# Projections of the three-branch attention units issued as one line of quarters at equal distances, tied to the attention's products on both sides

## Chip, cores and metric

The kernel runs on one core of a Trainium2 chip. The metric is the device time of one execution in microseconds (us): 919.52 us, the median of three runs (917.04 to 920.32).

## What is computed

One decoder layer over 1,024 tokens of width 1,024, in fp32. Cut to what matters:

```python
h = rms_norm(x, g_pre) * (1 + scale) + shift
proj = h @ w_in                 # split into q_a, three k/v pairs, gates, z_a, q_b, kv_b, z_b, merge
o_cmp, p_cmp = compressed_attention(qa, kc, vc)
o_slc = selected_attention(qa, ks_, vs_, select_blocks(p_cmp))
o_win = banded_attention(qa, kw_, vw_, window=512)
o_a = g0 * o_cmp + g1 * o_slc + g2 * o_win          # mixer A: 8 heads, three branches
y_a = (merge_heads(o_a) * silu(z_a)) @ w_o_nsa
o_b = banded_attention(qb, kb_, vb_, window=128, sinks)   # mixer B: 8 heads, one branch
y_b = (merge_heads(o_b) * silu(z_b)) @ w_o_swa
y = (sigmoid(m_a) * y_a + sigmoid(m_b) * y_b) @ w_out     # m_a, m_b: the merge gates
x = x + gate * rms_norm(y, g_post)
```

With 16 blocks of 64 keys and 16 selected, the selected branch (`slc`) is full causal attention.

## The kernel before

**Products.** An fp32 product is made of three fp32r products: each operand is split into a high and a low part (`hh`, `hl` for the normed input, `wh`, `wl` for weights, `ph`, `pl` for probabilities), and high times high, low times high and high times low are added in PSUM. The input's parts stay in SBUF for the whole kernel, as 8 pieces of 128 channels by two halves of 512 tokens.

**Projections.** One projection half (`proj_half`, lines 172 to 190) makes 128 output channels for 512 tokens: 8 pieces times 3 matmuls of 512 columns (lines 181, 188, 189) into one PSUM bank with the tag `pj` (two banks). Its weights come as a block in two halves: SyncE loads 256 KB (`wraw`, three buffers), ScalarE casts the high part (L155), GpSimd subtracts the low part (L158); `wh` and `wl` have six buffers, three blocks. What comes out is Q (scaled, split, L479), K (L494), Z (the SiLU gate, through a tanh, L522, to DRAM) or a merge gate (a copy by ScalarE, L859, to DRAM: "spilled").

**Attention.** It runs in four units: mixer B, groups 0 and 1 (one branch), then mixer A, groups 0 and 1 (three branches: `slc`, `win`, `cmp`). A unit goes through 8 blocks of 128 queries, branch by branch. `scores` makes, for each of 4 heads, products of Q and K (lines 752, 755) in one of three `s` banks, from which VectorE adds distances and takes minima (L762, L768); ScalarE then takes the exponential (L774), and GpSimd scales the rows (L786). One task later, `weigh` turns each 128 by 128 piece of the rows of 4 heads with four PE transposes into a `pt` bank (L821; two banks); ScalarE casts the high part `ph` (L827), VectorE subtracts the low part `pl` (L828), and PE multiplies the values with `ph` (L829) and with `pl` (L832) into the single `pv` bank. For the compressed branch that is L794, L800, L801 and L805. `finish` takes the block's output from the bank (L841, L842), multiplies it by Z and stores it.

**The order.** A scheduler that estimates times sets each engine's order when the program is built; the code steers it with priorities and with order-only dependencies (`after`, `chain`) that cost no semaphore. Attention is recorded at high priority. `mark` notes, at each attention product, how many columns of attention have been recorded so far (`done`, in microseconds at 2,400 columns each). Projections are recorded between tasks: Q, K and Z at steps that `spread` gives out, and the 28 merge halves by the shares in `LATE`, the fractions of them that each unit takes. A projection half is bound on one side: its first matmul must stand behind the attention product that was marked 3 us (`AHEAD`) before its place. Nothing says where it must be done; its 24 matmuls stand where the scheduler finds them best.

After the attention come two merge blocks that were kept back, the two output projections with their gates, and the last product.

Of the kernel before, what the change touches and what calls it, by code (L numbers as in the profile page):

```python
# [7 lines left out]
F32 = mybir.dt.float32  # L8
# [6 lines left out]
P = 128  # L15
D = 1024
S = 1024
HS = 512
KC = D // P
NT = S // P  # L20
EPS = 1e-6
LATE = (0.1, 0.1, 0.2, 0.6)
WARM = (7, 14, 8, 4)
KEEP = 2
WBUFS = 6
AHEAD = 3
PRIO = 1500
# [40 lines left out]
def hybrid_kernel(tc, io, out):  # L68
# [10 lines left out]
    def bank(tag):  # L79
        return ps.tile([P, 512], F32, tag=tag, name=f"b_{tag}", bufs=BANKS[tag])  # L80
# [15 lines left out]
    done = [0.0]  # L96

    def mark(ins, columns):

        marks.append((done[0], ins))  # L100
        done[0] += columns / 2400
# [365 lines left out]
    Q = {}  # L467
# [48 lines left out]
    def z_block(name, half, w):  # L516

        t = proj_half(w, half, lambda: bank("pj"))
        if half == 0:
            spilled[name] = dram.tile([P, S], F32, name=f"sp_{name}", tag=f"sp_{name}")  # L520
        sp = kq.tile([P, HS], F32, name="sp", tag="sp", bufs=1)
        nc.scalar.activation(sp, t, AF.Tanh, scale=0.5)  # L522
        nc.vector.scalar_tensor_tensor(sp, sp, 1.0, t, ALU.add, ALU.mult)
        nc.sync.dma_start(spilled[name][:, half * HS : half * HS + HS], sp)
# [148 lines left out]
    def chunks(lo, hi):  # L673
# [6 lines left out]
        return res  # L680

    cmp_scores = {}

# [10 lines left out]
    def scores(mixer, g, i, br):  # L694
# [33 lines left out]
        for r in range(4):  # L728
            h = 4 * g + r
            if len(rows) < 4:  # L730
                q = Q[(mixer, h, half)][:, qo : qo + P]
# [58 lines left out]
    def weigh_pairs(g, pairs, pv):  # L790

        t = bank("pt")
        for p in range(2):
# [15 lines left out]
    def weigh(mixer, g, i, br, tiles, pv, first, last):  # L809
# [6 lines left out]
        todo = [((b - b0) * P, V[b][:, vi]) for b in range(b0, i + 1)]  # L816
        for n, (off, v) in enumerate(todo):
            v = v.rearrange("p a d -> p (a d)")
            t = bank("pt")
# [29 lines left out]

    late = []  # L850

    def add_spill(name):
        def block(half, w):
            if half == 0:
                w.extend(load_block(name))
                spilled[name] = dram.tile([P, S], F32, name=f"sp_{name}", tag=f"sp_{name}")
            t = proj_half(w, half, lambda: bank("pj"))
            sp = kq.tile([P, HS], F32, name="sp", tag="sp", bufs=1)
            nc.scalar.copy(sp, t)  # L859
            nc.sync.dma_start(spilled[name][:, half * HS : half * HS + HS], sp)  # L860

        w = []
        for half in range(2):
            late.append(lambda half=half: block(half, w))

    for n in SPILL:
        add_spill(n)
    late_done = [0]
    n_late = len(late)

# [10 lines left out]
    for u, (mixer, g) in enumerate(units):  # L881
# [11 lines left out]

        own = [] if u == 1 else k_fills(mixer, g, 1)
        spread(own + q_fills(mixer, g, 1), 0, 3 * nt // 8)
        if u + 1 < len(units):
            m2, g2 = units[u + 1]
            if u == 2:
                spread(z_fills(m2, g2), 3 * nt // 8, nt)
            nk = k_fills(m2, g2, 0) if m2 == "A" else []  # L900
            spread(nk + q_fills(m2, g2, 0), nt // 2, nt)
        prev = None
        pvs = {}
# [9 lines left out]
        for n, (i, br) in enumerate(tasks):  # L913
# [13 lines left out]
            now = done[0] - begun  # L927
            while late_done[0] < n_late:

                part = ((late_done[0] + 0.5) / n_late - sum(LATE[:u])) / LATE[u]  # L930
                if part > 1 or part * whole[u] > now:
                    break
                hold[0] = held(begun + part * whole[u] - AHEAD)
                late.pop(0)()
                late_done[0] += 1
        with tc.high_priority(offset=PRIO):
            second(prev)
    for f in late:
        f()
    hold[0] = None  # L940
# [243 lines left out]
```

## Time and profile before

| | |
|---|---|
| median of three runs | 919.52 us (917.04 to 920.32) |
| the profiled execution's own time | 919.45 us |
| its span, first to last instruction | 917.6 us |
| TensorE (PE) busy | 902.7 us, 98% |
| weight loads (PEld) busy | 755.5 us, 82% |
| VectorE / ScalarE / GpSimd busy | 553.5 / 504.0 / 355.0 us |

PE's matmuls overlap in the records (a matmul of 512 columns is listed with some 390 ns while the next starts 0.23 us after it), so PE's busy share hides short stops; the starts of consecutive rows and the waits of the weight loads show them. Mixer B's units lie between about 165 and 316 us, mixer A's between 316 and 714 us: group 0 until about 495, group 1 from there.

### The profile page before, as it was taken

What the parts mean: (1) busy time and instruction counts of PE and PEld (TensorE: products, weight loads), DVE (VectorE), ACT (ScalarE), POOL (GpSimd) and SP (SyncE); (2) the same over time, 40 slices, a digit from 0 to 9 for tenths busy, and PEclk for the clock granted to TensorE, in tenths of its full rate; (3) what the DMA queues carried; (4) which work ended last, traced back from release to release, by engine and by line L of the source; (5) the groups of instructions that cost most, each with busy time, mean ns of one, the idle gap of its engine ahead of it and who ended that gap; (6) DMA issues with size and microseconds to landing.
All of it is one profiled execution on the core that took longest, in us unless ns stands there. A gap on an engine that the chain in (4) does not pass through costs nothing.

```text
span 917.6 us, 14306 instructions
## 1 busy us (share of the span) xinstructions
PE 902.7 (98%) x4568; PEld 755.5 (82%) x4568; DVE 553.5 (60%) x1546; ACT 504.0 (55%) x1151; POOL 355.0 (39%) x422
## 2 busy tenths in 40 slices
PE   9999999999999999999999999999999999999997
PEld 7888888888888878878887888887887888887885
DVE  5866863475677866785575865565555372676322
ACT  5476722466776675675565765665645465441111
POOL 0000421465675865553443764534433276200000
PEclk9999999999999999999999999999999999999999
DMA  8962442332242311202101221121211587334432
GB/s 320 304 242 75 139 161 72 127 96 95 79 118 90 112 62 44 83 26 70 64 30 35 81 86 61 37 72 39 77 47 49 185 260 240 109 110 178 138 98 85
DMA packets 63868, 100.82 MB, mean 110 GB/s; under 512 B 7473, under 2 KB 24241, under 8 KB 63794
## 3 DMA queue, kind: packets, MB, share of 16 engines
q1 hardware_dynamic: 62640, 98.69, 32.8%
q10 hardware_dynamic: 1154, 1.23, 0.4%
q8 instruction: 36, 0.59, 0.3%
q14 instruction: 38, 0.31, 0.1%
HBM read 79.97 MB, written 19.92 MB: 109 GB/s over the span
## 4 chain that ended last, share of the span: by engine, by line
PE 91%; DVE 3%; ACT 2%; issue 1%; DMA 1%; POOL 1%; DVEq 0%; ACTq 0%; POOLq 0%
PE b_pj L188 12%; PE b_pj L189 12%; PE b_pj L181 12%; PE b_pt L821 7%; PE b_s L752 4%; PE b_s L755 4%; PE b_pv L832 4%; PE b_pv L829 3%; PE b_s L1069 1%; PE b_s L1067 1%; PE b_s L1068 1%; PE b_pt L288 1%; DVE pl L828 1%; PE b_s L204 1%; PE b_s L990 1%
## 5 line engine op out<-in xcount | busy, mean ns | idle before, releaser
L181 PE MATMUL b_pj<-hh,wh 128*128 128x512 f32 x528 | 209.1, 396 | 0.0
L189 PE MATMUL b_pj<-hh,wl 128*128 128x512 f32 x528 | 208.5, 395 | 0.0
L188 PE MATMUL b_pj<-hl,wh 128*128 128x512 f32 x528 | 207.6, 393 | 0.0
L158 POOL TENSOR_TENSOR wl<-wraw,wh 128x512 fp32r<-128x512 f32 x102 | 133.9, 1316 | 138.6 <-ACT wh L155 92.6
L828 DVE TENSOR_TENSOR pl<-b_pt,ph 128x512 fp32r<-128x512 f32 x162 | 110.0, 685 | 46.3 <-ACT ph L827 45.4
L827 ACT CAST ph<-b_pt 128x512 fp32r<-128x512 f32 x162 | 92.8, 584 | 64.8 <-PE b_pt L821 51.2
L189 PEld LDWEIGHTS b_pj<-hh,wl 128*128 128x128 f32 x528 | 99.3, 188 | 18.5
L188 PEld LDWEIGHTS b_pj<-hl,wh 128*128 128x128 f32 x528 | 99.3, 188 | 17.8
L181 PEld LDWEIGHTS b_pj<-hh,wh 128*128 128x128 f32 x528 | 99.3, 188 | 17.6
L786 POOL TENSOR_SCALAR ps<-ps,rr,gates 128x128 f32<-128x128 f32 (+7 forms) x64 | 53.2, 836 | 98.9 <-DVE rr L778 92.3
L752 PE MATMUL b_s<-kh,q 128*128 128x256 f32 (+6 forms) x272 | 88.4, 332 | 1.5 <-DVE minc L768 0.9
L774 ACT ACTIVATE ps<-ps,mins 128x256 f32<-128x256 f32 (+7 forms) x96 | 65.1, 679 | 36.9 <-DVE mins L762 35.9
L755 PE MATMUL b_s<-kl,q 128*128 128x256 f32 (+6 forms) x272 | 84.2, 316 | 0.0
L155 ACT CAST wh<-wraw 128x512 fp32r<-128x512 f32 x94 | 58.0, 619 | 40.8 <-PE b_pj L188 32.9
L774 ACT ACTIVATE pw<-pw,mins 128x256 f32<-128x256 f32 (+4 forms) x96 | 60.5, 632 | 30.9 <-DVE mins L762 28.2
L832 PE MATMUL b_pv<-pl,V 128*128 128x512 f32 x162 | 69.6, 430 | 2.5 <-DVE pl L828 2.0
L829 PE MATMUL b_pv<-ph,V 128*128 128x512 f32 x162 | 67.2, 415 | 0.9 <-ACT ph L827 0.7
L786 POOL TENSOR_SCALAR pw<-pw,rr,gates 128x640 f32<-128x640 f32 (+4 forms) x64 | 47.6, 746 | 40.9 <-DVE rr L778 36.9
L843 POOL TENSOR_TENSOR ot<-ot,zt 64x512 f32<-64x512 f32 x32 | 41.3, 1290 | 49.3 <-DVE ot L842 40.0
L752 PEld LDWEIGHTS b_s<-kh,q 128*128 128x128 f32 x272 | 51.3, 188 | 10.7 <-DVE mins L762 2.7
L755 PEld LDWEIGHTS b_s<-kl,q 128*128 128x128 f32 x272 | 51.4, 189 | 5.8
L821 PE MATMUL b_pt<-ident,ps 128*128 128x128 f32 x344 | 55.4, 272 | 0.2 <-DVE pl L828 0.2
(292 smaller groups left out, 1842.0 us busy)
## 6 DMA issues: line engine op xcount, KB each, us to landing
wraw<-in_w_blk SPq DMA_DIRECT2D x90, 256.0 KB, 2.8
wa<-in_w_adaT SPq DMA_DIRECT2D x24, 512.0 KB, 5.2
w1raw<-in_w SPq DMA_DIRECT2D x16, 256.0 KB, 3.2
od<-ot SPq DMA_DIRECT2D x64, 64.0 KB, 2.1
sp_MA<-sp SPq DMA_DIRECT2D x16, 256.0 KB, 2.0
wraw<-in_w_o SPq DMA_DIRECT2D x16, 256.0 KB, 3.2
wraw<-in_w_out SPq DMA_DIRECT2D x16, 256.0 KB, 3.1
t<-od SPq DMA_DIRECT2D x16, 256.0 KB, 3.7
```

What stands on the lines that cost most here:

```text
L158: chain("wl", nc.gpsimd.tensor_tensor(wl, raw, wh.bitcast(F32), ALU.subtract))
L181: ins = nc.tensor.matmul(t, lhsT=wh, rhs=hh[kc][half], start=(kc == 0), stop=False)
L188: nc.tensor.matmul(t, lhsT=wh, rhs=hl[kc][half], start=False, stop=False)
L189: nc.tensor.matmul(t, lhsT=wl, rhs=hh[kc][half], start=False, stop=(kc == KC - 1))
L752: ins = nc.tensor.matmul(sp[:, :n_in], lhsT=q, rhs=rh, start=True, stop=False)
L755: nc.tensor.matmul(sp[:, :n_in], lhsT=q, rhs=rl, start=False, stop=True)
L774: nc.scalar.activation(rows[r][:, :off], rows[r][:, :off], AF.Exp, scale=-1.0, bias=last_min[:, r : r + 1], accum_out=sums[:, r : r + 1])
L786: nc.gpsimd.tensor_scalar(rows[r][:, :off], rows[r][:, :off], rr[:, r : r + 1], gate, ALU.mult, ALU.mult)
L821: ins = nc.tensor.transpose(t[:, r * P : r * P + P], rows[r][:, off : off + P], ident)
L828: nc.vector.tensor_tensor(pl, t, ph.bitcast(F32), ALU.subtract)
L829: ins = nc.tensor.matmul(pv, lhsT=v, rhs=ph, start=(first and n == 0), stop=False)
L832: nc.tensor.matmul(pv, lhsT=v, rhs=pl, start=False, stop=(last and n == len(todo) - 1))
```

## The change

In mixer A's two units, all projections of a unit (merge halves, its own K and Q for the second half of the tokens, for the first unit also Z of group 1 and the next unit's first K and Q) form one list, `line`. Each is cut into four quarters of 6 matmuls (2 of the 8 pieces), and the quarters are placed at equal distances over the attention's columns of the unit. `pump`, called before each head's scores and each transposed piece, records the quarters whose place has come. A quarter's first matmul is bound to stand behind the attention product of 3 us before its place, as before; new is that the first attention product marked at or after its place plus 4 us (`LAG`) must stand behind the quarter's last matmul (`owed`). A block's weights are loaded when the block before it in the line starts. Mixer B's units keep their way and take 3 merge halves each, as before. The first mixer A unit has 18 halves in its line (8 merge halves; 15 halves with 5 merge halves before), the second 17 (14 merge halves; 20 with 17 before). The instructions of every engine are the same in kind, shape and number.

```diff
-LATE = (0.1, 0.1, 0.2, 0.6)
+LATE = (0.1, 0.1)
+LAG = 4
...
+    owed = []
+
     def mark(ins, columns):
 
+        for o in [o for o in owed if o[0] <= done[0]]:
+            after(ins, o[1])
+            owed.remove(o)
         marks.append((done[0], ins))
         done[0] += columns / 2400
...
+    pieces = []
+
+    def pump():
+
+        while pieces and pieces[0][0] <= done[0]:
+            at, f = pieces.pop(0)
+            with tc.high_priority(offset=-PRIO):
+                f(at)
...
+    class Planned:
+
+
+        def __init__(self, name, half, out, w):
+            self.name, self.half, self.out, self.w = name, half, out, w
+
+        def load(self):
+            if not self.w:
+                self.w.extend(load_block(self.name))
...
+        def quarter(self, k, at, nxt):
+            if k == 0:
+                self.load()
+                if nxt:
+                    nxt.load()
+                self.t = bank("pj")
+            hold[0] = held(at - AHEAD)
+            for kc in (2 * k, 2 * k + 1):
+                wh, wl = (x[:, kc % KH, :] for x in self.w[kc // KH])
+                ins = nc.tensor.matmul(self.t, lhsT=wh, rhs=hh[kc][self.half], start=(kc == 0), stop=False)
+                if kc == 2 * k:
+                    chain("pj", ins)
+                    after(ins, hold[0])
+                nc.tensor.matmul(self.t, lhsT=wh, rhs=hl[kc][self.half], start=False, stop=False)
+                ins = nc.tensor.matmul(self.t, lhsT=wl, rhs=hh[kc][self.half], start=False, stop=(kc == KC - 1))
+            owed.append((at + LAG, ins))
+            if k == 3:
+                self.out(self.name, self.half, self.t)
...
-        own = [] if u == 1 else k_fills(mixer, g, 1)
-        spread(own + q_fills(mixer, g, 1), 0, 3 * nt // 8)
-        if u + 1 < len(units):
+        if mixer == "B":
+            own = [] if u == 1 else k_fills(mixer, g, 1)
+            spread(own + q_fills(mixer, g, 1), 0, 3 * nt // 8)
             m2, g2 = units[u + 1]
-            if u == 2:
-                spread(z_fills(m2, g2), 3 * nt // 8, nt)
             nk = k_fills(m2, g2, 0) if m2 == "A" else []
             spread(nk + q_fills(m2, g2, 0), nt // 2, nt)
+        else:
+            line = merges(2) + plan_k(g, 1) + plan_q("A", g, 1)
+            if u == 2:
+                for b in range(2):
+                    line += merges(2) + plan_z("A", 2 + b)
+                line += plan_k(1, 0) + plan_q("A", 1, 0) + merges(2)
+            else:
+                line += merges(len(late))
+            for n, f in enumerate(line):
+                nxt = next((x for x in line[n + 1 :] if x.w is not f.w), None)
+                for k in range(4):
+                    pieces.append((begun + whole[u] * (n + k / 4) / len(line),
+                                   lambda at, f=f, k=k, nxt=nxt: f.quarter(k, at, nxt)))
```

PE's order in the first mixer A unit, query block 4, where the `slc` branch ends (`V_131`, `V_132`, `V_133` are the values of key blocks 2, 3 and 4; `ps`, `pw` are rows of the two branches). Before:

```order
L821 MATMUL b_pt<-ident,ps 128x128 x4
L829 MATMUL b_pv<-ph,V_131 128x512
L832 MATMUL b_pv<-pl,V_131 128x512
L821 MATMUL b_pt<-ident,ps 128x128 x4
L829 MATMUL b_pv<-ph,V_132 128x512
L821 MATMUL b_pt<-ident,pw 128x128 x4
L832 MATMUL b_pv<-pl,V_132 128x512
L829 MATMUL b_pv<-ph,V_133 128x512
```

After (L841, L849 and L852 are the old L821, L829 and L832; L900, L904 and L905 are the three matmuls of a quarter's piece):

```order
L849 MATMUL b_pv<-ph,V_131 128x512
L852 MATMUL b_pv<-pl,V_131 128x512
L841 MATMUL b_pt<-ident,ps 128x128 x4
L900 MATMUL b_pj<-hh_87,wh 128x512
L904 MATMUL b_pj<-hl_103,wh 128x512
L905 MATMUL b_pj<-hh_87,wl 128x512
L900 MATMUL b_pj<-hh_89,wh 128x512
L904 MATMUL b_pj<-hl_105,wh 128x512
L905 MATMUL b_pj<-hh_89,wl 128x512
L849 MATMUL b_pv<-ph,V_132 128x512
L841 MATMUL b_pt<-ident,pw 128x128 x4
L852 MATMUL b_pv<-pl,V_132 128x512
```

Between a piece's transposes and the product that needs its cast now stand the six matmuls of a quarter; before, some 90 rows in a row around this place held no projection.

PE's order at the end of the second mixer A unit, the last `win` pieces (key blocks 3 to 7, `V_132` to `V_136`). Before:

```order
L829 MATMUL b_pv<-ph,V_132 128x512
L832 MATMUL b_pv<-pl,V_132 128x512
L821 MATMUL b_pt<-ident,pw 128x128 x4
L829 MATMUL b_pv<-ph,V_133 128x512
L832 MATMUL b_pv<-pl,V_133 128x512
L821 MATMUL b_pt<-ident,pw 128x128 x4
L829 MATMUL b_pv<-ph,V_134 128x512
L832 MATMUL b_pv<-pl,V_134 128x512
```

After:

```order
L849 MATMUL b_pv<-ph,V_136 128x512
L841 MATMUL b_pt<-ident,pw 128x128 x4
L852 MATMUL b_pv<-pl,V_136 128x512
L849 MATMUL b_pv<-ph,V_132 128x512
L852 MATMUL b_pv<-pl,V_132 128x512
L841 MATMUL b_pt<-ident,pw 128x128 x4
L849 MATMUL b_pv<-ph,V_133 128x512
L852 MATMUL b_pv<-pl,V_133 128x512
L841 MATMUL b_pt<-ident,pw 128x128 x4
L849 MATMUL b_pv<-ph,V_134 128x512
L852 MATMUL b_pv<-pl,V_134 128x512
```

Here the order is the same in kind: the line's last quarter stands just ahead of `V_136` of the `slc` branch, and the last five pieces follow one another without a projection, in both kernels.

## Rows read from the trace of the kernel before

**Rows 1.** The page's first part: busy time of each engine, its share of the span and the number of its instructions.

```profile
PE 902.7 (98%) x4568; PEld 755.5 (82%) x4568; DVE 553.5 (60%) x1546; ACT 504.0 (55%) x1151; POOL 355.0 (39%) x422
```

**Rows 2.** Busy time by stretch (us from the span's start): PE, PEld, DVE, ACT and POOL with the number of instructions, then the granted TensorE clock, the DMA share and GB/s. The first row is a stretch of mixer B's units, the others are of mixer A's.

```profile
200.00:300.00 100.00, 100.00 (x533) 85.02 (x532) 65.94 (x199) 68.43 (x186) 61.81 (x82) 1.00 0.32 97
324.00:330.00 6.00, 4.92 (x22) 2.95 (x21) 5.88 (x25) 5.37 (x16) 4.03 (x5) 1.00 0.15 46
384.00:410.00 26.00, 24.82 (x145) 19.59 (x144) 22.16 (x89) 21.74 (x57) 16.42 (x23) 1.00 0.12 41
410.00:453.00 43.00, 43.00 (x224) 36.35 (x224) 22.61 (x71) 23.52 (x51) 18.33 (x20) 1.00 0.17 56
480.00:497.00 17.00, 15.54 (x90) 11.80 (x89) 11.52 (x46) 11.59 (x29) 7.67 (x13) 1.00 0.10 31
693.00:714.00 21.00, 20.01 (x106) 15.33 (x105) 9.60 (x21) 10.13 (x20) 4.34 (x4) 1.00 0.21 63
```

**Rows 3.** Who waited for whom, the weight loads (PEld) alone, from 316 to 716 us: total us, times, the longest.

```profile
PEld b_pv L832 <- DVE pl L828: 7.2, 17, 0.5
PEld b_s L752 <- DVE mins L762: 2.7, 9, 0.6
PEld b_pv L829 <- ACT ph L827: 2.7, 8, 0.6
PEld b_pt L821 <- issue: 2.5, 7, 0.4
PEld b_s L752 <- PE b_s L755: 1.5, 2, 1.2
PEld b_pv L805 <- ACT ph L800: 1.1, 1, 1.1
PEld b_s L752 <- issue: 0.8, 2, 0.4
PEld b_pt L821 <- DVE pl L828: 0.7, 3, 0.3
PEld b_pv L829 <- DVE ot L842: 0.5, 1, 0.5
PEld b_pv L829 <- issue: 0.3, 1, 0.3
```

**Rows 4.** The timeline of PE: start, duration, operation. Two matmuls of a projection in a row, and four transposes between other work.

```profile
333.00 0.39 PE L181 MATMUL b_pj<-hh,wh 128*128 128x512 f32 x1
333.23 0.39 PE L188 MATMUL b_pj<-hl,wh 128*128 128x512 f32 x1
...
337.06 0.60 PE L821 MATMUL b_pt<-ident,ps 128*128 128x128 f32 x4
337.42 0.47 PE L181 MATMUL b_pj<-hh,wh 128*128 128x512 f32 x1
337.73 0.39 PE L188 MATMUL b_pj<-hl,wh 128*128 128x512 f32 x1
```

**Rows 5.** The timeline of several engines in a stretch without projections: one weighing from its transposes to its two products; in brackets the idle time before, and what ended it.

```profile
456.31 1.26 ACT L827 CAST ph<-b_pt 128x512 fp32r<-128x512 f32 x2 [1.49 <-PE b_pt L821]
456.35 0.60 PE L821 MATMUL b_pt<-ident,ps 128*128 128x128 f32 x4
456.93 1.37 DVE L828 TENSOR_TENSOR pl<-b_pt,ph 128x512 fp32r<-128x512 f32 x2 [1.28 <-ACT ph L827]
456.95 0.50 PE L829 MATMUL b_pv<-ph,V 128*128 128x512 f32 x1
...
457.68 0.50 PE L832 MATMUL b_pv<-pl,V 128*128 128x512 f32 x1 [0.22 <-DVE pl L828]
```

**Rows 6.** The timeline at the longest of the waits for ScalarE.

```profile
387.48 0.60 ACT L155 CAST wh<-wraw 128x512 fp32r<-128x512 f32 x1
...
387.80 0.33 PE L755 MATMUL b_s<-kl,q 128*128 128x384 f32 x1
387.99 0.57 ACT L859 COPY sp<-b_pj 128x512 f32<-128x512 f32 x1
...
388.47 0.36 ACT L800 CAST ph<-b_pt 128x256 fp32r<-128x256 f32 x1
...
388.89 0.50 PE L805 MATMUL b_pv<-ph,vc 128*128 128x256 f32 x2 [0.76 <-ACT ph L800]
```

**Rows 7.** The same view as rows 3, from 693 to 714 us, the end of the second mixer A unit.

```profile
PEld b_pv L832 <- DVE pl L828: 2.7, 6, 0.5
PEld b_pv L829 <- ACT ph L827: 0.6, 2, 0.3
```

**Rows 8.** The same view from 568 to 572 us.

```profile
PEld b_s L752 <- DVE mins L762: 0.6, 2, 0.3
PEld b_pt L821 <- issue: 0.4, 1, 0.4
PEld b_pv L829 <- ACT ph L827: 0.3, 1, 0.3
```

**Rows 9.** The same view from 660 to 666 us.

```profile
PEld b_pv L832 <- DVE pl L828: 0.5, 1, 0.5
```

**Rows 10.** The page's fifth and sixth parts: the two steps that make a weight block's parts, with the time that their engine sat idle before them and for what, and the load itself (KB each, median us from issue to landing).

```profile
L158 POOL TENSOR_TENSOR wl<-wraw,wh 128x512 fp32r<-128x512 f32 x102 | 133.9, 1316 | 138.6 <-ACT wh L155 92.6
L155 ACT CAST wh<-wraw 128x512 fp32r<-128x512 f32 x94 | 58.0, 619 | 40.8 <-PE b_pj L188 32.9
wraw<-in_w_blk SPq DMA_DIRECT2D x90, 256.0 KB, 2.8
```

More of the change, by code (lines that the diff above doesn't have):

```diff
@@ L516, in z_block, with z_out @@
     def z_block(name, half, w):
-        t = proj_half(w, half, lambda: bank("pj"))
+        z_out(name, half, proj_half(w, half, lambda: bank("pj")))
+    def z_out(name, half, t):
         if half == 0:
@@ L729, in scores @@
             h = 4 * g + r
+            pump()
             if len(rows) < 4:
@@ L790, in weigh_pairs @@
     def weigh_pairs(g, pairs, pv):
+        pump()
         t = bank("pt")
@@ L817, in weigh @@
         for n, (off, v) in enumerate(todo):
+            pump()
             v = v.rearrange("p a d -> p (a d)")
@@ L848, in finish @@
                 ot[:, 256 * p : 256 * p + 256].rearrange("d (r t) -> d r t", r=2))
[L850 to L860, printed above, removed]
-        w = []
-        for half in range(2):
-            late.append(lambda half=half: block(half, w))
@@ L866, in hybrid_kernel, with spill_out, whole @@
-    for n in SPILL:
-        add_spill(n)
+    def spill_out(name, half, t):
+        if half == 0:
+            spilled[name] = dram.tile([P, S], F32, name=f"sp_{name}", tag=f"sp_{name}")
+        sp = kq.tile([P, HS], F32, name="sp", tag="sp", bufs=1)
+        nc.scalar.copy(sp, t)
+        nc.sync.dma_start(spilled[name][:, half * HS : half * HS + HS], sp)
+    class Planned:
[4 more added lines that the diff above has]
+                self.w.extend(load_block(self.name))
+        def whole(self):
+            self.load()
+            self.out(self.name, self.half, proj_half(self.w, self.half, lambda: bank("pj")))
+        def quarter(self, k, at, nxt):
+            if k == 0:
+                self.load()
+                if nxt:
[13 more added lines that the diff above has]
+                self.out(self.name, self.half, self.t)
@@ new lines, in both, with plan_q, plan_k, plan_z @@
+    def both(name, out):
+        w = []
+        return [Planned(name, half, out, w) for half in range(2)]
+    def plan_q(mixer, g, half):
+        return [Planned(f"Q{mixer}{g}{p}", half, lambda name, half, t, p=p: q_block(mixer, g, p, half, None, t), [])
+                for p in range(2)]
+    def plan_k(g, half):
+        return [Planned(f"KA{g}", half, lambda name, half, t: k_block([("slc", g), ("win", g)], half, None, t), [])]
+    def plan_z(mixer, b):
+        return both(f"Z{mixer}{b}", lambda name, half, t: z_out(name, half, t))
@@ L868, in hybrid_kernel, with merges @@
+    late = [f for name in SPILL for f in both(name, spill_out)]
+    n_late = len(late)
     late_done = [0]
-    n_late = len(late)
+    def merges(n):
+        return [late.pop(0) for _ in range(n)]
     units = [("B", 0), ("B", 1), ("A", 0), ("A", 1)]
@@ L927, in hybrid_kernel @@
             now = done[0] - begun
-            while late_done[0] < n_late:
+            while mixer == "B":
                 part = ((late_done[0] + 0.5) / n_late - sum(LATE[:u])) / LATE[u]
@@ L933, in hybrid_kernel @@
                 hold[0] = held(begun + part * whole[u] - AHEAD)
-                late.pop(0)()
+                late.pop(0).whole()
                 late_done[0] += 1
@@ L937, in hybrid_kernel @@
             second(prev)
-    for f in late:
-        f()
+        for at, f in pieces:
+            f(at)
+        pieces.clear()
     hold[0] = None
```

## The prediction, on record before the changed kernel ran

> **What bounds the kernel now.** I read the share of each engine first: PE is busy 98% of the span, every other engine under 61% [rows 1]. So only PE's own time can shrink, and since the change leaves every instruction as it is, only its stops can. The busy share hides those: the records overlap, and two projection matmuls of 512 columns start 0.23 us apart though each is listed with 0.39 [rows 4]. What a stop looks like I took from the timeline. In [rows 5] the product with `ph` starts at 456.95 and the one with `pl` at 457.68: 0.73 us for a matmul that takes 0.23, so 0.50 us lost, behind the transposes, a cast on ScalarE and a subtraction on VectorE. The weight load of the second product shows this wait, so the waits of the weight loads measure the loss, and in mixer A's units they add up to 20.0 us over the ten rows of [rows 3].
>
> Where they lie is told by the table of stretches [rows 2]. In a stretch of mixer B's units PE is 100% busy and the weight loads 85%; so they are from 410 to 453, and the view of waits has nothing for the weight loads in either. In 324 to 330 the loads fall to 49% (2.95 of 6 us), in 384 to 410 to 75%, in 480 to 497 to 69%, in 693 to 714 to 73%. Set beside PE's order, these are the places where no projection stands: weighing pieces and scores follow one another, each needs an answer from ScalarE or VectorE, and PE has nothing else to do. The longest, 384 to 410, holds some 20 us of attention work without one projection matmul.
>
> **The change, part by part.**
>
> *Instructions.* Kind, shape and number are the same on every engine, and the waits attached to PE's are about as many. An order-only dependency costs nothing. This part is 0. Fifteen projection halves in the first mixer A unit become 18, twenty in the second become 17; a half is 24 matmuls of 0.23 us [rows 4], 5.5 us, so some 16 us of work cross the border between the units and come back on the other side. The sum of that is 0 as well.
>
> *The dry stretches.* I costed PE's order with [rows 4]: 0.23 us for 512 columns, shorter ones in proportion to their columns, and 0.11 us for a transpose (four start at 337.06, the next two matmuls at 337.42 and 337.73, so 0.67 us for four transposes and a matmul of 0.23). Then I measured each run of attention work between two projection matmuls. Before, mixer A has nine such runs of over 4 us (20.0, 11.6, 8.3, 6.4, 6.3, 6.2, 5.4, 4.7 and 4.1), together 73 us. After, one is left: 5.0 us, at the very end, where the line's quarters have run out. The runs of 2.5 to 4 us become more: ten before, 15 after. Everything else is shorter.
>
> The same from the other side: a weighing needs 1.33 us from its first transpose to its second product (456.35 to 457.68, [rows 5]), of which the transposes and the first product fill 0.67; so 0.66 us of other work is needed between. In mixer A before, 20 of some 130 second products have under 1.6 us of PE's work between the last transpose and themselves; after, 4, all of them in that last run. A quarter puts 6 x 0.23 = 1.4 us in between, more than the 0.66.
>
> *What it gives.* I take the loss as 19 us rather than 20.0, since part of a load's wait lies under the matmul before it: at 387.80 the listed wait of the load is 1.1 us [rows 3], while PE's starts are 1.09 us apart where 0.17 us would do [rows 6], so 0.92 lost. What stays: (a) the end. Before, 693 to 714 holds two runs, 6.3 and 4.1 us, and 2.7 + 0.6 = 3.3 us of waits [rows 7], 0.32 us for each us of run; 5.0 us of run after the change keeps 1.6. (b) the 15 runs of 2.5 to 4 us. Of ten like them before, two lost anything that the view shows: one 1.3 us (568 to 572, [rows 8]) and one 0.5 [rows 9], so 0.18 us each on average, 2.7 for 15. (c) new stops. None is in sight, but VectorE's and ScalarE's own order moves too; the bounds are 0 and about 8 (below), and I take 0.7, since stretches with even projections show none. Gain: 19 - 1.6 - 2.7 - 0.7 = 14.0 us. Against the profiled execution's own 919.45 us, which is 0.07 from the median of the runs, that is 905.5.
>
> *What is moved and must stay hidden.* Weights: a block's load is recorded when the block before it starts. From the load to the low part takes 2.8 + 0.62 + 2 x 1.3 = 6.0 us plus what stands ahead in the queues [rows 10]; by the orders of ScalarE and PE the smallest lead of a high part's cast on its first use is 18 us of PE's work in mixer A, 19 before. That covers it; if the cover went, each late block would stop PE outright. GpSimd's low parts are waited for by nobody on PE in [rows 3]. SyncE issues the same transfers. Queries: the last quarter of the second Q block now ends 6.1 us of PE's work ahead of the first scores that read it; ScalarE's and VectorE's split lies in that. In mixer B's units the smallest such gap is 5.1 us, and PE is 100% busy there [rows 2], so 0. The single `pv` bank: between a query block's last product and the next one's first, at least 1.9 us of PE's work after and 2.1 before; that wait is in the trace once, with 0.5 us (`ot`, [rows 3]). It may come two to four times: 0 to 2 us, inside (c). The clock: 1.00, its 2.4 GHz level, in every stretch of [rows 2], the one without projections included.
>
> **The rivals.**
>
> *The queues keep their waits (half the gain).* Placed on PE's order, some 11 of the 19 us stand where too little PE work lies between need and answer; the other 8 stand where there is 2 us of work or more but the answering engine had something else first. [Rows 6] shows one: the cast for the compressed branch starts at 388.47 because a weight cast and the copy of a merge half stood ahead of it. Those casts and copies are still there, and scores still come in bunches of three heads. For it: bunches stay. Against it: such waits appear only inside dry stretches; the same engines at 66% and 68% in mixer B's units stop PE nowhere [rows 2]. If all 8 stay, on top of (a) and (b) less what these share, the gain is 9 to 10 us: 910.
>
> *The waits move (no change).* The 4 us limit makes quarters come at equal distances whether or not PE needs filling there; stops could turn up at the bunches of scores instead, for `mins` (2.7 us before, [rows 3]), and at the end. That would need some 14 us of new stops, five times what `mins` costs today. 917 to 920.
>
> *A slower kernel: weights late.* Place: GpSimd's low part at a block's first quarter, with the attention behind it held by the new limit, so that nothing can pass. It decides from the point where a block comes over 18 us later than the order thinks. The two lines use 22 blocks; at 0.64 us each the stops eat the gain, at 1 us each the time is 919.45 - 14 + 22 = 927. Against it: GpSimd idles 92.6 us in all for the cast ahead of its part [rows 10], so the part is made as soon as it can be.
>
> *A slower kernel: the clock.* All stretches have 1.00 today. If a twentieth of mixer A's 398 us ran at the 1.2 GHz level, the same work would take 20 us longer: 919.45 - 14 + 20 = 925. The Trainium skill (Perfetto Trace Analysis, Matmul Optimizations) says that the matmul engine scales its power with its utilization, "so it's important that matmuls execute back-to-back in batches", and this change cuts batches of 24 into batches of 6. By that rule the finer mixture is a risk; the trace does not bear it out, since the stretch with the fewest batches, 384 to 410, is at 1.00.
>
> **How the numbers follow.** The forecast case, 905.5, gets 0.68; half the gain, 910, 0.18; no change 0.09; the two slower ones 0.03 and 0.02. Everything recovered is the lower bound: 919.45 - 19 = 900.5. The upper end reaches past the half-gain case with the bounds of (c): 913. That leaves about 0.15 outside, above. Changes of under 0.5% (4.6 us) are about what a measurement of this kernel cannot tell from none, its three runs spreading over 3.3 us. Faster by more than that, under 914.9: 0.87 (the first two cases and a little of the third); within: 0.09; slower: 0.04.
>
> **What would show it.** Right: the weight loads' waits in mixer A's units under 6 us in total, mostly in the last 10 us before the attention ends; the loads busy 83 to 85% in every stretch between; the first mixer A unit still ending near 497 us (three halves more, some 12 us fewer stops), the second some 14 us earlier than 714; everything behind it the same length; the clock 1.00. Wrong: waits of PE for `wl` or `wh`, for `q`, or rows for `mins` and `ph` of 8 us and more spread evenly over the units, or a granted clock under 1.00.

## The result, and the profile after

The changed kernel takes 908.29 us (median of four runs, 907.7 to 909.31); the kernel before, with the runs made beside it, 918.78 us (917.04 to 920.32). The ratio is 0.9887, its 95% interval 0.9866 to 0.9909: 10.5 us faster, inside the predicted range, 2.8 us above the predicted 905.5. The profiled executions differ by 10.1 us (spans 917.6 and 907.5).

In the page's first part nothing speaks of it but PE's busy time [rows 1]:

```profile
PE 894.1 (99%) x4568; PEld 755.8 (83%) x4568; DVE 554.3 (61%) x1546; ACT 505.3 (56%) x1151; POOL 352.8 (39%) x422
```

The table of stretches, columns as in [rows 2]; the stretches of mixer A between those shown (316 to 335 and 495 to 536 us) have PE busy throughout and the clock at 1.00:

```profile
200.00:300.00 100.00, 100.00 (x534) 85.20 (x533) 66.02 (x198) 68.28 (x187) 62.06 (x82) 1.00 0.32 98
335.00:339.00 4.00, 1.90 (x11) 1.21 (x10) 3.83 (x13) 2.23 (x4) 1.58 (x2) 1.00 0.02 6
339.00:495.00 156.00, 156.00 (x847) 132.25 (x845) 102.61 (x351) 100.06 (x226) 76.18 (x85) 1.00 0.19 60
536.00:540.00 4.00, 2.02 (x13) 1.24 (x11) 3.81 (x12) 2.27 (x4) 1.61 (x2) 1.00 0.02 8
540.00:693.00 153.00, 153.00 (x831) 129.99 (x830) 92.94 (x322) 95.04 (x213) 72.36 (x82) 1.00 0.18 59
693.00:703.00 10.00, 9.59 (x53) 7.28 (x52) 5.06 (x8) 4.90 (x9) 1.42 (x2) 1.00 0.24 79
```

Between 339 and 693 us, but for four microseconds, mixer A now looks as mixer B does: PE always busy, its loads 85% busy (132.25 of 156, 129.99 of 153) where [rows 2] had 49% to 75% in places. What is left is in three short stretches. The waits of the weight loads from 316 to 702 us say for what (total us, times, the longest). Line numbers moved: L841 are the transposes of a weighing, L847 and L848 the cast `ph` and the subtraction `pl`, L849 and L852 the two products, L861 and L862 the copy and the addition that empty the `pv` bank at a query block's end, L770 and L773 the scores.

```profile
PEld b_pv L849 <- DVE ot L862: 4.0, 2, 2.0
PEld b_pt L841 <- issue: 1.4, 2, 0.7
PEld b_pv L852 <- DVE pl L848: 0.6, 2, 0.5
PEld b_pt L813 <- DVE pl L848: 0.5, 1, 0.5
PEld b_pt L841 <- DVE pl L848: 0.3, 1, 0.3
PEld b_s L770 <- DVE mins L780: 0.2, 1, 0.2
```

With one more wait for `pl`, which ends at 702.35 us, its row is 1.2 and the sum 7.6 us, against 20.0 in [rows 3]. The waits for `pl`, 7.2 and 0.7 us before, are 2.0, those for `mins` fell from 2.7 to 0.2, and those for `ph`, 3.8 before, are gone. The 4.0 us for `ot` are more than the 0.5 of [rows 3]: a wait that grew. One of its two, from the timeline of all engines (brackets: idle time before, and what ended it; rows in order of start, L500 to L511 are the split of a K block's keys into parts and copies of them):

```profile
333.65 0.67 DVE L508 TENSOR_TENSOR kl<-b_pj,kh 64x512 fp32r<-64x512 f32 x1
334.35 0.42 DVE L510 CAST kh<-kh 64x512 fp32r<-64x512 f32 x1
334.35 0.58 ACT L500 CAST kh<-b_pj 64x512 fp32r<-64x512 f32 x1 [2.50 <-DVE kl L508]
334.69 0.41 DVE L511 CAST kl<-kl 64x512 fp32r<-64x512 f32 x1
334.96 0.59 ACT L861 COPY ot<-b_pv 64x512 f32<-64x512 f32 x1
335.00 0.60 PE L841 MATMUL b_pt<-ident,ps 128*128 128x128 f32 x4
335.12 0.23 DVE L504 CAST kl<-kl 128x128 fp32r<-128x128 f32 x1
335.48 0.69 DVE L508 TENSOR_TENSOR kl<-b_pj,kh 64x512 fp32r<-64x512 f32 x1
336.20 0.42 DVE L510 CAST kh<-kh 64x512 fp32r<-64x512 f32 x1
336.66 0.68 DVE L862 TENSOR_TENSOR ot<-b_pv,ot 64x512 f32<-64x512 f32 x1
337.39 0.50 PE L849 MATMUL b_pv<-ph,V 128*128 128x512 f32 x1 [1.80 <-DVE ot L862]
```

The line's second projection is a K block (`plan_k`, right behind the first merge block), and its keys are ready just as a query block ends. Their rows on VectorE stand in one piece ahead of the addition (L862) that frees the `pv` bank; on ScalarE the copy (L861) that the addition needs stands behind a cast of keys that itself idled 2.50 us for VectorE's first subtraction. PE starts at 335.00 and then at 337.39; four transposes are 0.44 us of it [rows 4], so 1.95 us are lost, and 0.47 more behind it. The same happens at 536 us with the second unit's K block: 4.8 us in all.

The piece is longer than its rows would be alone. It begins with a copy of keys (L503) at 331.44 us, and at 532.51 us in the second unit, that takes 1.68 us each time beside a GpSimd instruction; where no GpSimd instruction runs beside it, the same copy takes 0.21 to 0.23 us in all twelve traces (last section). Worked back along VectorE's order, the addition would have come up to 1.45 us earlier without this, which is an estimate: no run takes the two apart.

Behind the attention nothing moved: the last `pl` product starts at 702.35 us (712.44 before), and from there to the span's end it is 205.15 us (205.16 before).

**A second measure.** From the first score to the last `pl` product PE runs the same 3,256 instructions in both kernels. That way is 622.1 us long before (90.35 to 712.44) and 611.5 after (90.85 to 702.35): 10.6 us shorter. Of it 10.1 arrive in the span, since the first score starts 0.5 us later.

### The profile page after: what moved, and what is told of

The parts are those of the page before. It is cut to its first block, busy times and chain, and to the rows that moved or that the text cites. A ratio compares the mean times of both kernels' runs of the same rounds, so it can differ in the third digit from the quotient of the medians.

```text
span 907.5 us, 14317 instructions
## 1 busy us (share of the span) xinstructions
PE 894.1 (99%) x4568; PEld 755.8 (83%) x4568; DVE 554.3 (61%) x1546; ACT 505.3 (56%) x1151; POOL 352.8 (39%) x422
## 4 chain that ended last, share of the span: by engine, by line
PE 94%; DVE 3%; ACT 1%; issue 1%; DMA 0%; POOL 0%; DVEq 0%; POOLq 0%; ACTq 0%
PE b_pt L841 8%; PE b_pj L900 7%; PE b_pj L904 7%; PE b_pj L905 7%; PE b_pj L194 5%; PE b_pj L195 5%; PE b_pj L187 5%; PE b_s L773 4%; PE b_s L770 4%; PE b_pv L852 4%; PE b_pv L849 4%; PE b_s L1140 1%; PE b_s L1139 1%; PE b_s L1141 1%; PE b_pt L294 1%; PE b_s L210 1%
## 5 line engine op out<-in xcount | busy, mean ns | idle before, releaser
L848 DVE TENSOR_TENSOR pl<-b_pt,ph 128x512 fp32r<-128x512 f32 x162 | 110.3, 686 | 55.5 <-ACT ph L847 54.6
L847 ACT CAST ph<-b_pt 128x512 fp32r<-128x512 f32 x162 | 93.5, 584 | 63.5 <-PE b_pt L841 52.7
L900 PE MATMUL b_pj<-hh,wh 128*128 128x512 f32 x288 | 117.1, 410 | 0.0
L905 PE MATMUL b_pj<-hh,wl 128*128 128x512 f32 x288 | 113.8, 395 | 0.0
L904 PE MATMUL b_pj<-hl,wh 128*128 128x512 f32 x288 | 113.3, 395 | 0.0
L187 PE MATMUL b_pj<-hh,wh 128*128 128x512 f32 x240 | 94.5, 394 | 0.0
L770 PE MATMUL b_s<-kh,q 128*128 128x256 f32 (+6 forms) x272 | 85.8, 322 | 0.0
L773 PE MATMUL b_s<-kl,q 128*128 128x256 f32 (+6 forms) x272 | 83.8, 316 | 0.0
L849 PE MATMUL b_pv<-ph,V 128*128 128x512 f32 x162 | 65.5, 404 | 3.5 <-DVE ot L862 3.5
L852 PE MATMUL b_pv<-pl,V 128*128 128x512 f32 x162 | 67.9, 419 | 0.3
L905 PEld LDWEIGHTS b_pj<-hh,wl 128*128 128x128 f32 x288 | 54.1, 188 | 10.8
L904 PEld LDWEIGHTS b_pj<-hl,wh 128*128 128x128 f32 x288 | 54.3, 189 | 8.8
L900 PEld LDWEIGHTS b_pj<-hh,wh 128*128 128x128 f32 x288 | 53.8, 189 | 7.8
```

The costliest lines, as they stand in the source:

```text
L187: ins = nc.tensor.matmul(t, lhsT=wh, rhs=hh[kc][half], start=(kc == 0), stop=False)
L770: ins = nc.tensor.matmul(sp[:, :n_in], lhsT=q, rhs=rh, start=True, stop=False)
L773: nc.tensor.matmul(sp[:, :n_in], lhsT=q, rhs=rl, start=False, stop=True)
L848: nc.vector.tensor_tensor(pl, t, ph.bitcast(F32), ALU.subtract)
L852: nc.tensor.matmul(pv, lhsT=v, rhs=pl, start=False, stop=(last and n == len(todo) - 1))
L900: ins = nc.tensor.matmul(self.t, lhsT=wh, rhs=hh[kc][self.half], start=(kc == 0), stop=False)
```

## The experiments

Theory: the time lost is the sum of PE's stops in mixer A; the change removes those that dry stretches make, and gives some 5 us back at two borders, because the K block's rows stand ahead of `ot`. Rivals: the limit on the far side of the quarters, or the new share of work between the units, makes the gain; the border stop comes from too little PE work there (1.9 us), whatever VectorE does. One rival has no experiment of its own: that the stop comes from the copy held beside GpSimd, and not from the block's rows as such. All kernels below change a few lines. Ratios are to the kernel before, run beside them. The waits are the weight loads' sum from 284 to 725 us of the profiled execution.

| kernel | median us | ratio (95%) | span profiled | waits | span less waits |
|---|---|---|---|---|---|
| before | 918.78 | 1 | 917.6 | 20.0 | 897.6 |
| the change | 908.29 | 0.9887 (0.9866 to 0.9909) | 907.5 | 7.6 | 899.9 |
| no_limit | 909.12 | 0.9887 (0.9870 to 0.9904) | 907.1 | 7.9 | 899.2 |
| share | 919.96 | 0.9995 (0.9980 to 1.0011) | 918.1 | 20.6 | 897.5 |
| halves | 926.89 | 1.0077 (1.0057 to 1.0097) | 925.8 | 27.0 | 898.8 |
| dry20 | 920.92 | 1.0014 (1.0000 to 1.0028) | 919.0 | 17.8 | 901.2 |
| k_last | 907.83 | 0.9874 (0.9854 to 0.9894) | 905.4 | 7.2 | 898.2 |
| k_pool | 904.85 | 0.9835 (0.9812 to 0.9858) | 900.9 | 3.8 | 897.1 |
| k_first | 914.88 | 0.9942 (0.9920 to 0.9963) | 912.8 | 11.8 | 901.0 |
| best3 | 913.81 | 0.9934 (0.9914 to 0.9954) | 913.2 | 11.6 | 901.6 |
| pool_last | 904.68 | 0.9838 (0.9819 to 0.9857) | 902.4 | 2.5 | 899.9 |
| pool_last_t5 | 906.15 | 0.9850 (0.9831 to 0.9870) | 904.8 | 4.5 | 900.3 |

The last column is the theory's account: over waits of 2.5 to 27.0 us and spans of 901 to 926, what remains stays between 897 and 902.

**The limit on the far side alone (no_limit).**

```diff
-LAG = 4
+LAG = 1e9
```

> The changed kernel without the limit on the far side: no attention product is made to wait behind a quarter's last matmul. Quarters, places and the limit on the near side stay. Theory (equal distances of small pieces are what fills the runs; the scheduler puts a quarter where its place is without being told): PE's order has the same runs without projections (one over 4 us, at the end) and the same K copies ahead of ot: 908 us, within 1. Rival (the limit on the far side holds the quarters apart): some dry runs return, 911 us or more.

The time is that of the change, and so is the stop at the borders:

```profile
PEld b_pv L849 <- DVE ot L862: 4.0, 2, 2.1
```

The limit does nothing here: the near side's hold and the priorities already place the quarters.

**The share between the units alone (share),** on the kernel before, with its halves placed as they were:

```diff
-LATE = (0.1, 0.1, 0.2, 0.6)
+LATE = (0.1, 0.1, 0.3, 0.5)
```

> The kernel before with one line changed: the shares of the merge halves are (0.1, 0.1, 0.3, 0.5) instead of (0.1, 0.1, 0.2, 0.6), so that the two mixer A units carry the projection work about as evenly as in the changed kernel (three merge halves moved from the second to the first), with nothing cut or bound. PE's order then has 15 runs of over 4 us of attention work without a projection, 4.8 to 8.4 us, 95 us together (73 before, 5 after the change). Theory (what counts is the runs): no gain, 918 us or more; by the 0.25 to 0.37 us of stops per us of such runs that the kernel before and the kernel with whole halves show, 24 to 35 us of stops in place of 20, 923 to 934 us. Rival (the even share between the units brings the gain): 908 to 913 us.

No gain, and no loss either: waits from 284 to 725 us of the same kind and size as [rows 3], led by

```profile
PEld b_pv L832 <- DVE pl L828: 7.7, 19, 0.5
```

So the gain is not in the share. Its dry runs came to 95 us, yet the waits to 20.6: the loss per us of run is no constant, and with it the higher of the times expected falls.

**Whole halves at equal distances (halves).** Each block's four quarters get the same place; count and share are those of the change.

```diff
-                    pieces.append((begun + whole[u] * (n + k / 4) / len(line),
+                    pieces.append((begun + whole[u] * n / len(line),
```

> The changed kernel with the four quarters of a half recorded at one place, so 24 matmuls at a time, the halves at equal distances and the limits as they are. PE's order then has 13 runs of attention work over 4 us without a projection, 4.1 to 6.9 us each, 72 us together (73 us in nine runs in the kernel before). Theory (a run of over 4 us stops PE for about 0.25 us per us, as the kernel before shows: 18.1 us of waits in 73 us): 18 us of stops in place of 7.2, 919 us, no faster than the kernel before. Rival (equal distances are enough, at whatever grain; what hurts is only the very long runs of 8 to 20 us): 904 to 909 us.

Slower than the kernel before, run beside it (919.89), by 7.0 us, which is what its waits have more (27.0 - 20.0). From 316 to 712 us the largest are

```profile
PEld b_pv L852 <- DVE pl L848: 7.6, 17, 1.2
PEld b_s L770 <- DVE minc L786: 4.3, 3, 3.0
PEld b_s L770 <- DVE mins L780: 2.7, 6, 0.9
```

Whole halves at equal distances are thus worse than the placement before; the cut into quarters is what helps at equal distances. Quarters that the scheduler places freely, as it did the halves before, were not run. The rate that I had taken, 0.25 us lost per us of dry run, was too low: 27.0 us over the 72 us of runs that were expected is 0.36. Not all of that is the runs' own: the longest wait, 3.0 us for `minc`, follows copies of a K block that take 0.96 and 1.48 us, beside GpSimd again, where 0.42 is usual.

**The same dry runs put back (dry20).** The line is squeezed into the first 80% of each unit, so that its end is dry.

```diff
-                    pieces.append((begun + whole[u] * (n + k / 4) / len(line),
+                    pieces.append((begun + 0.8 * whole[u] * (n + k / 4) / len(line),
```

> The changed kernel with all quarters of a unit placed in the first 80% of its attention, so that the last fifth of each unit has none: two runs of 20.6 and 22.7 us in PE's order. Theory (0.25 us of stops per us of such a run): 10.8 us of stops in them; with the two stops for the pv bank of the changed kernel (4.9 us) if they stay, 912 to 917 us. Rival (attention alone can feed PE; the stops of the kernel before came from the bursts of projection evacuations and weight casts beside it, which are absent in these runs): 905 to 908 us.

The two runs, 20.6 and 22.7 us, lose 5.1 and 9.2 us in waits: 0.33 per us, 14.3 in all, more than the whole gain of the change. The time, 920.92, is above what was expected. Two things add to it that the kernel before does not have, both in the second run (table of stretches):

```profile
695.00:698.40 3.40, 0.44 (x4) 0.20 (x2) 2.32 (x13) 3.35 (x11) 3.40 (x6) 1.00 0.01 2
699.20:703.00 3.80, 3.79 (x13) 3.07 (x14) 1.41 (x3) 1.52 (x4) 1.94 (x3) 0.57 0.25 69
```

In the first PE works 0.44 of 3.40 us while ScalarE is busy throughout, since a `ph` cast stands behind exponentials in its queue (the longest wait for `ph` there is 3.3 us, against 1.1 in [rows 3]). In the second the granted clock is 0.57 on average, and 13 instructions of PE take 3.8 us.

**The K block last among its unit's own blocks (k_last).**

```diff
-            line = merges(2) + plan_k(g, 1) + plan_q("A", g, 1)
+            line = merges(2) + plan_q("A", g, 1) + plan_k(g, 1)
```

> The line of each mixer A unit starts with two merge halves, the two Q halves and then K, instead of two merge halves, K and the two Q halves; nothing else. In VectorE's order of the changed kernel eight copies and subtractions of the K block stand right ahead of the addition that frees the pv bank (ot), at one query block border of each unit, and PE stops there for 2.0 and 1.9 us, plus 0.5 us each right behind. With K last, none of them is among the ten rows ahead of any such addition, while PE's work between the query blocks at these borders stays 1.9 us. Theory (the K block's evacuation is what is late): both stops go, 908.3 - 4.9 = 903.4 us. Rival (1.9 us of PE's work between two query blocks is too short by itself, whatever stands in VectorE's order): the stops stay, 908 us.

The wait for `ot` is gone, though the `pv` bank's border is still 1.9 us of PE's work: the rival "too little work at the border" falls. But the time hardly moved. The K rows on VectorE stop another product where they now lie; from the timeline:

```profile
357.32 0.69 DVE L508 TENSOR_TENSOR kl<-b_pj,kh 64x512 fp32r<-64x512 f32 x1
357.65 0.42 PE L849 MATMUL b_pv<-ph,V 128*128 128x512 f32 x1
358.05 0.42 DVE L510 CAST kh<-kh 64x512 fp32r<-64x512 f32 x1
358.39 0.42 DVE L511 CAST kl<-kl 64x512 fp32r<-64x512 f32 x1
358.84 1.29 DVE L848 TENSOR_TENSOR pl<-b_pt,ph 128x512 fp32r<-128x512 f32 x2
359.68 0.74 PE L841 MATMUL b_pt<-ident,pw 128*128 128x128 f32 x4 [1.61 <-DVE pl L848]
362.35 0.63 PE L900 MATMUL b_pj<-hh,wh 128*128 128x512 f32 x1
362.77 0.63 PE L904 MATMUL b_pj<-hl,wh 128*128 128x512 f32 x1
```

The subtraction `pl` starts at 358.84, behind the K block, and PE's transposes, which need its bank, at 359.68: 1.8 us lost, and the same at 559.86 us. The last two rows start 0.42 us apart where [rows 4] has 0.23, because of this, in the table of stretches:

```profile
357.00:359.70 2.70, 0.86 (x6) 0.47 (x4) 2.61 (x7) 0.00 (x0) 0.00 (x0) 1.00 0.55 134
359.70:363.60 3.90, 3.90 (x15) 3.27 (x16) 3.23 (x14) 2.90 (x6) 0.88 (x1) 0.56 0.08 26
560.00:562.00 2.00, 0.39 (x3) 0.14 (x2) 1.94 (x5) 0.00 (x0) 0.00 (x0) 1.00 0.49 145
562.00:566.00 4.00, 4.00 (x23) 3.42 (x23) 3.50 (x15) 3.27 (x8) 0.88 (x1) 1.00 0.03 11
```

After the first stop PE has 15 instructions in 3.9 us at a granted clock of 0.56, about 1.6 us lost; after the second 23 in 4.0 us at 1.00. So the block costs where it meets attention, not at the border alone. Here too one of its copies is held: the first L511 of each block, some 4 us ahead of the stop, takes 2.75 us instead of 0.42 beside two GpSimd instructions.

**Less of the block on VectorE (k_pool).** Its copies for the other head go to GpSimd, 1.7 us less on VectorE for each block. Blocks in mixer B's units that are placed by the order move too, not those of mixer A alone.

```diff
-            dve(nc.vector.tensor_copy(kh[o0:o1, :], hi.bitcast(F32)))
-            dve(nc.vector.tensor_copy(kl[o0:o1, :], lo.bitcast(F32)))
+            if hold[0] is None:
+                dve(nc.vector.tensor_copy(kh[o0:o1, :], hi.bitcast(F32)))
+                dve(nc.vector.tensor_copy(kl[o0:o1, :], lo.bitcast(F32)))
+            else:
+                nc.gpsimd.tensor_copy(kh[o0:o1, :], hi.bitcast(F32))
+                nc.gpsimd.tensor_copy(kl[o0:o1, :], lo.bitcast(F32))
```

> The changed kernel with the two duplicating copies of each K head pair (L510, L511 of the changed kernel, 0.42 us each on VectorE, four of them per K block) done by GpSimd in mixer A's lines; places as in the changed kernel. VectorE's rows of the K block shrink by 1.7 us, from about 4.6. Theory (a K block's rows on VectorE keep it from freeing the pv bank and from making pl; the stop is as long as they are): the stops for ot fall from 4.0 us to 1 or less, 905 us. Rival 1 (ScalarE's cast of the second head pair, which waits for VectorE's first subtraction, is what holds ot, so the copies do not matter): 908 us. Rival 2 (GpSimd's copies are slower and the scores of the new K come late): 910 us or more.

The time falls by 3.4 us to 904.85, as expected, and so does the way from the first score to the last `pl` product (611.5 to 608.1); the waits fall from 7.6 to 3.8; the largest from 316 to 702 us (lines four higher than in the change):

```profile
PEld b_pv L853 <- DVE ot L866: 2.1, 2, 1.1
PEld b_pv L856 <- DVE pl L852: 1.2, 3, 0.5
```

A shorter block, a shorter stop: 4.0 to 2.1 us. I had expected 1 or less; two subtractions and the copies of the earlier keys still stand there, and the copy L503 is held at 1.68 us in both blocks as before.

**The K block first (k_first); with k_pool and more room at the end (best3).** k_first:

```diff
-            line = merges(2) + plan_k(g, 1) + plan_q("A", g, 1)
+            line = plan_k(g, 1) + merges(2) + plan_q("A", g, 1)
```

best3 is this and k_pool's edit, with the last unit's line drawn out by 3 us:

```diff
-                    pieces.append((begun + whole[u] * (n + k / 4) / len(line),
+                    pieces.append((begun + (whole[u] + 3 * (u == 3)) * (n + k / 4) / len(line),
```

> The line of each mixer A unit starts with K, then two merge halves and the two Q halves. In VectorE's order no K row stands among the ten ahead of an addition that frees the pv bank, but for four at the start of the second unit. With K last the stops moved from ot to the transposes that wait for pl (3.6 us of 4.0). Theory (a K block's rows stop PE wherever they come as one block): some stop of 1 to 2 us per unit stays, for pl or mins: 905 to 908 us. Rival (early in the unit, with few keys per query block, the attention asks little of VectorE, so they pass unnoticed): 903.5 us.

> K first, its duplicating copies on GpSimd, and in the second mixer A unit the quarters stretched by 3 us of attention columns, so that they reach the end: PE's order has no run over 3.8 us without a projection. Theory: of the 7.6 us of weight loads' waits in the changed kernel's mixer A units the 4.0 for ot and most of the last 2 us go, 902 to 904 us. Rival (GpSimd's copies or the first quarters come late): 907 us or more.

Both missed: 914.88 and 913.81. At a unit's start a query block has little work for PE, and the block of K rows meets scores that wait for minima. Waits of k_first from 284 to 725 us: the two largest of the weight loads, which do not name the minima, the largest of the matmuls behind those loads, which does, and a stretch behind such a stop:

```profile
PEld b_s L770 <- PE b_pt L841: 2.2, 3, 0.9
PEld b_s L770 <- issue: 1.9, 6, 0.4
PE b_s L770 <- DVE minc L786: 2.5, 4, 0.9
```

```profile
521.60:525.50 3.90, 3.84 (x12) 3.08 (x13) 2.26 (x16) 3.33 (x16) 3.40 (x8) 0.56 0.16 63
```

Here, too, the mean clock is 0.56 over 3.9 us, and best3 has a stretch like it (0.50 from 328.05 to 331.40 us). By the table's account the waits of 11.8 us (11.6 in best3) explain most of the loss, and the clock adds to it. Neither loss is the block's rows alone. In k_first the scores at 519.92 us start 1.2 us after those before them, and ahead of the minima that they wait for stands a K copy (L510, 517.50 us) that takes 1.67 us instead of 0.42, beside a GpSimd instruction once more. In best3 the longest wait of a matmul, 1.7 us for `ot` at 327.01 us, has no K row ahead of it: ScalarE's copy (L865, 325.56 us) had idled 2.20 us until the block's output before, in the same buffer, was stored.

**Both helps together (pool_last), and the end drawn out (pool_last_t5).** pool_last has the edits of k_pool and of k_last; pool_last_t5 adds `5 * (u == 3)` where best3 has 3.

> The kernel with GpSimd's K copies, and K behind the two Q halves in each line. Of the two stops for ot that are left there (2.1 us of the weight loads' waits) nothing should stay, since no K row stands ahead of such an addition. Theory (the stop is as long as the K rows in one block on VectorE, wherever they meet the attention): with K last and all copies on VectorE they cost 1.8 us of pl at two places; without the four copies (1.7 us) nearly nothing: waits of 2 us in all, at the end, 903 us. Rival (what is left of the K rows costs as much at the new place): 905 us.

> The same, with the second unit's quarters stretched by 5 us of attention columns, so that the last ones stand at the end of the attention: PE's order has no run over 4.2 us (5.0 at the end before). Theory: the 1.5 us of waits in the last 10 us go, 901.5 to 902.5 us, and the weight loads' waits in mixer A's units are under 1 us. Rival (as with K first and the same stretch, the moved places bring dry runs and stops elsewhere): 905 us or more.

Waits from 284 to 725 us, the largest of pool_last, then of pool_last_t5:

```profile
PEld b_pv L856 <- DVE pl L852: 1.2, 3, 0.5
PEld b_pv L853 <- ACT ph L851: 0.8, 2, 0.4
```

```profile
PEld b_pv L853 <- ACT ph L851: 1.5, 2, 1.1
PEld b_pt L845 <- POOL kh L514: 1.4, 1, 1.4
```

pool_last has no wait for `ot` and the fewest waits of all, 2.5 us, near the 2 that were expected; yet 904.68 us cannot be told from k_pool's 904.85 and is the time of the rival. In the profiled executions the way from the first score to the last `pl` product is shorter by 1.8 us (606.3 against 608.1), but it began later, at 91.27 against 87.97 us; those first 90 us are the same work in both. In pool_last_t5 the waits for `pl` at the end shrink to 0.8 us, and transposes now wait 1.4 us for GpSimd's copy of keys (L514): 1.5 us slower than pool_last, as its rival said. The best versions are k_pool and pool_last, some 15 us under the kernel before, and 3.5 (by the medians) to 5 us (by the ratios) under the change.

## Why the prediction was right, step by step

- **Only PE's stops can shrink, and the weight loads' waits measure them.** Shown, by the account over twelve kernels, to within the 4.6 us by which its last column spreads. The instructions' count is the same and the part behind the attention took the same time.
- **19 us of loss.** Somewhat too high. 10.6 us were recovered on the way from the first score to the last product, and some 7.0 stay (4.8 at the borders, 1.7 at the end, 0.5 between), so 17 to 18.
- **(a) the end, 1.6 us.** Right: the `pl` waits of the last ten microseconds sum to 1.7 (three of L852 with 1.2, one of L813 with 0.5), in 7.28 of 10 us of loads.
- **(b) the 15 runs of 2.5 to 4 us, 2.7 us.** Wrong in size: the stretches that hold nearly all of them have PE 100% busy and two small waits, 0.3 us for `pl` and 0.2 for `mins`; 0.5 us at most. The price came from two rows of the kernel before, [rows 8] and [rows 9], which lay beside longer runs; that the other engines were behind there already is my reading, not tested.
- **(c) new stops, 0.7 us.** The step that failed: 4.8 us. The place was named (the `pv` bank between query blocks, "0 to 2 us"), but it was priced by the one row of `ot`, 0.5 us in [rows 3], and by PE's work there. What was left out is VectorE's own order: the K block's rows, some 4.6 us, spread among others before (at 377.91 to 382.88 us, beside projections), now lie in one piece ahead of the addition. k_last shows that the border alone makes no such stop, k_pool that the stop shrinks with the piece. How much of it is the copy held beside GpSimd, 1.68 us of the piece at both borders where 0.23 is usual, stays open. My bound of 8 us held it.
- **Sum.** Against a gain of 14.0: -1.4 on the base, -0.1 by (a), +2.2 by (b), -4.1 by (c) and -0.5 ahead of the first score make 10.1, and the profiled executions give 10.1. That (b) and (c) partly covered for each other is luck: the time came nearer than the terms.
- **Shares of the gain.** The change is three things. Two of them, alone or taken away, move nothing (share, no_limit); quarters instead of halves at the same distances are worth 18.6 us (926.89 to 908.29).
- **The rivals.** *Queues keep half the gain*, 910: its time is near, its mechanism is not: the waits for `pl`, `ph` and `mins` fell from 14.4 to 2.2 us, with bunches of scores as before. *Waits move*, 917 to 920: not so here, but k_first, with the same quarters, shows the mechanism: 6.7 of its 11.8 us of waits are those of scores. *Weights late*: no weight load waits for `wl`, `wh` or `q`. *The clock*: 1.00 in every stretch after the change. By the rule cited from the Trainium skill (Perfetto Trace Analysis, Matmul Optimizations) the finer mixture should have been a risk; in these traces it was none: batches of 6 ran at 1.00 throughout the attention (908.29 us), and so did batches of 24 (halves, 926.89 us), so the clock does not tell the two apart. Where the clock fell during the attention, in four other variants, it followed stops of PE.
- **What would show it.** The loads at 85%, the clock and the length of what comes behind held; the first unit's last addition came at 511.3 us (513.5 before), near its old place as said. The waits under 6 us did not hold (7.6), nor their place (most lie at the two borders), and the second unit ended 10.1 us earlier, not 14.

## What to carry to other kernels

Where PE waits on short chains over other engines, fill between need and answer with independent matmuls in small pieces (here 1.4 us of work where 0.66 us was needed; other sizes than this and halves were not run); the same filling in larger pieces at even distances can be worse than no plan. When the filler's results are post-processed on another engine, its whole block of rows is a new obstacle in that engine's order: look up what stands behind it and which of its rows run beside another engine that slows them, and move part of it elsewhere or shorten it before moving it about. A busy share of 98% can hide 2%; the sum of the weight loads' waits shows it.

## What the runs showed of the hardware

The means of 0.56 and 0.57 above are stretches at two levels: cut closer, the granted clock is 0.50 (1.2 GHz) from 360.10 to 363.40 us in k_last, from 699.10 to 702.45 in dry20, from 522.00 to 525.35 in k_first and from 328.05 to 331.40 in best3, and 1.00 (2.4 GHz) around it. Each lies behind stops of PE: one of 2.0 us between starts in k_last (357.65 to 359.68 us), 3.5 us in dry20 (695.00 to 698.48), several shorter ones in k_first and best3 (the longest 1.2 and 2.0 us between starts). Equal stops left it at 1.00: k_last's second (559.86 to 561.89), the change's own two of 2.4 us between starts, and this one in halves, 0.66 us of work in 3.4:

```profile
550.00:553.40 3.40, 0.66 (x6) 0.42 (x4) 3.34 (x8) 2.11 (x4) 1.78 (x2) 1.00 0.39 124
553.40:557.00 3.60, 3.33 (x16) 2.39 (x17) 3.54 (x14) 1.95 (x6) 1.28 (x1) 1.00 0.10 33
```

So the length of the stop alone does not decide; what does stays open.

A copy on VectorE can take eight times as long beside GpSimd. The first row of the piece that stops PE at 335 us, 0.21 us at its fastest, and the longest such copy of k_last, 0.42 us as a rule:

```profile
331.44 1.68 DVE L503 CAST kh<-kh 128x128 fp32r<-128x128 f32 x1
331.75 1.29 POOL L164 TENSOR_TENSOR wl<-wraw,wh 128x512 fp32r<-128x512 f32 x1
353.26 1.53 POOL L863 TENSOR_TENSOR ot<-ot,zt 64x512 f32<-64x512 f32 x1
353.57 2.75 DVE L511 CAST kl<-kl 64x512 fp32r<-64x512 f32 x1
354.75 1.28 POOL L164 TENSOR_TENSOR wl<-wraw,wh 128x512 fp32r<-128x512 f32 x1
```

Over the twelve traces there are 132 of the 128x128 copies. The 71 with no GpSimd instruction beside them took 0.21 to 0.23 us. The 30 that took over 0.3 us all had one beside them, and 29 of them ended within 0.1 us of the end of a GpSimd instruction. The 208 copies of 64x512 say the same: 0.41 to 0.43 us for the 141 without one, and the 30 over 0.5 us all had one and ended 0.27 to 0.29 us from its end. Having one beside it is not enough (31 and 37 copies were not slowed so), and no run moved GpSimd's instruction alone, so the traces show the pairing and not its cause.
